# Prompt scores from float32r parts, one tile for both score banks, and a first layer with six equal PSUM banks

## The chip, the cores and the metric

The kernel runs on one core of one Trainium2 chip. The metric is the device time of one execution in microseconds (us). Three runs of the kernel before give a median of 1257.61 us (1257.02 to 1259.03). Inside the core, TensorE (PE, with weight loads as PEld), VectorE (DVE), ScalarE (ACT) and GpSimd (POOL) run side by side; SyncE (SP) issues most of the loads. PE writes into PSUM, which has eight banks; DVE and ACT read the results out of them.

## The reference, cut to what matters

Two layers run over a prompt of 512 tokens and 64 sample tokens (8 sequences of 8), so 576 columns in all, 1024 features wide. Each layer is `x + gate(c) * Mixer(RMSNorm(x) * (1 + scale(c)) + shift(c))`; shift, scale and gate come from `silu(c) @ ada_w + ada_b` (the conditioning). Layer 0 is a gated linear recurrence; layer 1 is attention with three groups of dilation 1, 4 and 16. For the prompt, in one group:

```
s = einsum('brihd,brjhd->brhij', q, k) * ATT_SCALE - slopes * (diff * dil)
s = where(valid, s, NEG_INF)
lse = logsumexp(s); p = exp(s - lse)
o = einsum('brhij,brjhd->brihd', p, v)
```

The three groups are joined by a softmax over their `lse`, which equals one softmax over all scores of the three groups. The new k and v rows of the prompt are outputs too, as are the recurrence's states. All of it is in float32.

## The kernel before

A product of two float32 matrices is made from parts: H is the value rounded to float32r (an ACT copy, line 148), L is the rest (a DVE subtraction, line 149), and PE sums H·H, H·L and L·H in three float32r matmuls. So each weight tile of 128 columns costs 8 k-tiles × 3 products × 2 halves (256 prompt columns; 256 prompt and 64 sample columns) = 48 matmuls in `project` (line 182). Matmuls on plain float32 operands stand in the trace as two matmul records each.

**First layer.** The conditioning is made in parts of 512 columns by `ada_part`: two rounds (`q` = 0 and 4) of four float32 matmuls at line 245, each on one k-tile of `ada_w`, then a DVE copy (line 215) and four small transposing matmuls (line 218). The parts of the shift and scale of layer 0 stand at the start. With `project_wide` (line 201) the first three weight tiles of the layer are accumulated beside them, k-tile by k-tile, as the modulated input `hH`, `hL` appears. Then twelve input tiles go through a convolution on DVE (`xb_group`), the gates (`gates`, line 494: matmuls into the `sc` banks, a sigmoid on ACT, then exp, tanh, sqrt on ACT and a scan on DVE, line 512), and a gating by twelve further tiles (`gb_group`). Eight further conditioning parts are called one by one between these groups by `next_ada`, a whole part each time. Then `lru_w_out` is applied (line 182 with `YH`, `YL`), the residual and the next norm follow.

**Second layer.** For each pair of heads (hp, 8 of them) nine weight tiles give q, k and v in three groups; q and k stay in tiles `qk`, features on partitions, so the two heads lie on partitions 0 to 63 and 64 to 127. `prompt_att` goes through four blocks B of 128 queries. For each head (hh) it writes the scores of group 0 (line 793, 256 keys, or 128 in block 0, float32) and of groups 1 and 2 (line 798, 32-row pieces, float32) into a bank `sc`. DVE adds the bias (lines 805, 808) and finds the maximum (line 810), ACT takes exp (line 811), PE transposes (lines 816, 818) and multiplies with v (line 826). The sample attention (`sample_att`) runs in small steps between the weight tiles, and its scores use the `sc` banks as well.

**PSUM and order.** The eight banks: `mm` 2, `tp` 2, `sc` 2, `pvp` 1, `pvs` 1. In the first layer `project` goes round `mm`, `mm`, `pvp`, `pvs`. The order on each engine is made by a scheduler from the order of the code, a priority mark (`tc.high_priority`) and its own timing model; each engine then runs its list strictly in order, and an instruction that waits holds up all behind it on its engine.

Of the kernel before, what the change touches and what calls it, by code (L numbers as in the profile page):

```python
# [26 lines left out]
TAB_W = 512 + S_W + 256 + 32 + 4 + 32 + 32 + 4 + 8 + 32 + 16  # L27
QK_BUFS = 10
# [9 lines left out]
def shape_consts():  # L38
# [41 lines left out]
    hm = 0.5 * ((np.arange(256) // 64)[None, :] == h4)  # L80
# [7 lines left out]
def kernel(  # L88
# [16 lines left out]
    def bank(tag, bufs, name):  # L105
        return ps.tile([128, 512], F32, name=name, tag=tag, bufs=bufs)

    mm_tags = ["mm", "mm", "pvp", "pvs"]
    mm_next = [0]

    def mm_bank():
        tag = mm_tags[mm_next[0] % len(mm_tags)]
        mm_next[0] += 1
        return bank(tag, 2 if tag == "mm" else 1, tag)


    tp_bank = lambda: bank("tp", 2, "tp")
    sc_bank = lambda: bank("sc", 2, "sc")
    pv_bank = lambda tag="pvp": bank(tag, 1, tag)

# [65 lines left out]
    def project_wide(raws, xs):  # L186

        pts = []
        for o in range(3):
            a = bank("mm", 2, "mm") if o < 2 else pv_bank("pvp")  # L190
            b = sc_bank() if o < 2 else pv_bank("pvs")
            pts.append((a[:, 0:256], b[:, 0:320]))
        n = len(xs)
        for q in range(0, n, 4):
            ws = [split_w(r[:, q:q + 4], 4, xs[q:q + 4])[0] for r in raws]
            for k, (XH, XL) in enumerate(xs[q:q + 4]):
                for o, (H, L, _) in enumerate(ws):
                    for half in range(2):
                        c0, c1 = CHUNKS[half]
                        for i, (a, b) in enumerate(((H, XH), (H, XL), (L, XH))):  # L200
                            T.matmul(pts[o][half], a[:, k], b[:, c0:c1], start=(q + k == 0 and i == 0),
                                     stop=(q + k == n - 1 and i == 2))
        return pts
# [29 lines left out]
    def ada_part(pool, l, f0, f1, kstep=1, abufs=4):  # L233

        pt = sc_bank()
        for q in (0, 4):
# [10 lines left out]
            with tc.issue_after(lead.ins):  # L247
                for j in range(3):
                    part(j)
        if l == 1 and f0 >= 16:  # L250
            ada_rows(pool, pt, f0)
        else:
            ada_mod(pool, l, pt, f0, f1)

# [103 lines left out]


# [19 lines left out]
    for c in range(4):  # L379
        ada_part(sp, 0, 2 * c, 8 + 2 * c, 2, 12)  # L380
        if c == 1:
            raw0 = [load_raw(lru_w_in[0, :, 128 * j:128 * (j + 1)], 8) for j in range(3)]
        for kt in (2 * c, 2 * c + 1):
            xn = sp.tile([128, NT], F32, name="xn", tag="xn", bufs=2)
            h = sp.tile([128, NT], F32, name="hmod", tag="hmod", bufs=2)
            G.tensor_tensor(xn, xT[:, kt], bc, ALU.mult)
            modulate(h, 0, kt, xn)
        if c == 3:
            nc.sync.dma_start(xs_dram[0], xT)
    wide0 = project_wide(raw0, hX)  # L390
# [20 lines left out]
    def xb_group(g, wide=None):  # L411
# [32 lines left out]
        if wide:  # L444
            def wide_evac(o, pts):
                prep(o)
                for half in range(2):
                    make(o)(half, pts[half])
                conv(o)
            for o, pts in enumerate(wide):  # L450
                wide_evac(o, pts)
        else:
            for o in range(3):
                j = 3 * g + o
                prep(o)
                project(load_w(lru_w_in[0, :, 128 * j:128 * (j + 1)], 8, hX), make(o))
                conv(o)
# [19 lines left out]
    def gates(g, xs):  # L477
# [39 lines left out]
    def gb_group(g, hs):  # L517
# [3 lines left out]
        for o in range(3):  # L521
# [8 lines left out]
            split(hs[:, o], YH[:, o], YL[:, o])  # L530
        return [(YH[:, o], YL[:, o]) for o in range(3)]

    adas = [(0, 16, 18), (0, 20, 22)] + [(1, 2 * c, 8 + 2 * c) for c in range(4)] + [(1, 16, 18), (1, 20, 22)]

    def next_ada(n=1):
        for _ in range(n):
            if adas:
                ada_part(lp, *adas.pop(0))

    yX = []  # L540
    x0 = xb_group(0, wide0)
    x1g = xb_group(1)
    m0 = gates(0, x0)
    next_ada()
    x2 = xb_group(2)
    m1 = gates(1, x1g)
    next_ada()
    yX += gb_group(0, m0)
    next_ada()
    x3 = xb_group(3)  # L550
    m2 = gates(2, x2)
    next_ada()
    yX += gb_group(1, m1)
    next_ada()
    m3 = gates(3, x3)
    next_ada()
    yX += gb_group(2, m2)
    next_ada(2)
    yX += gb_group(3, m3)
    warm = lp.tile([128, 1], F32, name="warm")  # L560
# [78 lines left out]
    mm_tags[:] = ["mm"]  # L639
# [7 lines left out]
    for w in (512, S_W, 256, 32, 4, 32, 32, 4, 8, 32, 16):  # L647
# [29 lines left out]
    def tnt():  # L677
        return ap.tile([128, NT], F32, name="qk", tag="qk", bufs=QK_BUFS)
# [25 lines left out]
    def qkv(hq, KN, VN, qs, q, k, tok):  # L704

        def make(hp, g, c):
            hpi = hp % 2
            dst = t512("vT", 2) if c == 2 else tnt()

            def pevac(half, pt):  # L710
                cs = slice(256 * half, 256 * half + 256)
                if c == 0:
                    S.activation(dst[:, cs], pt[:, 0:256], AF.Copy, scale=0.125)
                else:
                    order = "p (b s r) -> p b r s" if g == 0 else "p (r b s) -> p b r s"
                    evac(dst[:, 0:NP].rearrange(order, b=4, r=4)[:, 2 * half:2 * half + 2],
                         pt[:, 0:256].rearrange("p (b r s) -> p b r s", b=2, r=4))
# [7 lines left out]
        def after(hp, g, c, dst):  # L725
# [6 lines left out]
            if g == 0:  # L732
# [8 lines left out]
                else:  # L741
                    T.transpose(tp[:, 0:128], dst[:, 384:512], eye)
# [22 lines left out]
        if hq == 0:  # L765
            def wide_evac(o, pts):
                dst, f = make(0, 0, o)
                for half in range(2):
                    f(half, pts[half])
                after(0, 0, o, dst)  # L770
            raws = [load_raw(att_w_in[0, :, 1024 * c:1024 * c + 128], 8) for c in range(3)]
# [489 lines left out]
```

## Time and profile before

| | |
|---|---|
| median of three runs | 1257.61 us |
| the profiled execution | 1252.48 us, of which the span of the instructions is 1250.7 us |
| PE, DVE, ACT busy | 1182.4, 844.9, 448.7 us |
| PE share of the chain that ended last | 82% |
| mean granted clock of PE | 0.969 of full speed |

The span is the time from the first to the last instruction of the program; the rest of the execution lies around it. The chain that ended last is found backwards from the last instruction: at each step to what released it, or to the instruction before it on its engine. A stretch that it spends on a DMA or on "issue" is time in which PE stood still. The granted clock of PE has two levels, 1.2 and 2.4 GHz; 1.00 means that the upper one held throughout the stretch.

### The profile page before, as it was taken

To read this page: it belongs to the slowest core of one execution; us is meant where nothing else is said; L and a number is where in the kernel's file an instruction comes from. 1 tells how busy PE (TensorE), PEld (TensorE's weight loads), DVE (VectorE), ACT (ScalarE), POOL (GpSimd) and SP (SyncE) were. 2 spreads that over 40 slices of the span, in tenths; PEclk is the share of its full clock that TensorE was granted. 3 is DMA by queue.
4 is the path that set the end of the run, shared out by engine and by line. 5 is a ranking of instruction groups with operands and counts; after the bars stand their busy time and mean duration, and the time that the engine had idled before them with its cause. 6 is when DMAs were issued, how large, how long until landed. Compare 5 with 4: busy or idle time off the path is not lost.

```text
span 1250.7 us, 25771 instructions
## 1 busy us (share of the span) xinstructions
PE 1182.4 (95%) x10344; PEld 1038.2 (83%) x10344; DVE 844.9 (68%) x1609; ACT 448.7 (36%) x895; POOL 219.2 (18%) x299
## 2 busy tenths in 40 slices
PE   6989899898997999899999999999999999999897
PEld 4789889786897998797998897988887988897775
DVE  6585894835437349885588765687774777776645
ACT  4167566552322323233222333223232223233421
POOL 3234453522110201020010030020020100030000
PEclk9899999997997999899999999999999999999899
DMA  9742253445540488482699481999671997484912
GB/s 302 232 117 89 82 169 91 147 125 178 156 137 27 128 225 224 131 241 79 181 262 237 132 243 52 251 252 203 185 199 56 269 255 173 124 231 145 239 55 76
DMA packets 242565, 209.51 MB, mean 168 GB/s; under 512 B 15324, under 2 KB 224956, under 8 KB 242318
## 3 DMA queue, kind: packets, MB, share of 16 engines
q1 hardware_dynamic: 229218, 172.73, 50.5%
q10 hardware_dynamic: 8124, 23.61, 6.4%
q0 software_dynamic: 5104, 11.52, 3.1%
q8 instruction: 82, 1.34, 0.5%
q14 instruction: 37, 0.30, 0.1%
HBM read 188.94 MB, written 18.87 MB: 166 GB/s over the span
## 4 chain that ended last, share of the span: by engine, by line
PE 82%; DMA 7%; DVE 6%; issue 2%; ACT 2%; SPq 0%; POOL 0%; ACTq 0%; DVEq 0%; POOLq 0%
PE mm L182 44%; PE mm L1191 4%; PE pvs L182 4%; PE pvp L182 4%; PE pvs L1011 3%; PE sc L494 3%; PE sc L793 3%; PE sc L798 2%; PE pvp L826 2%; PE sc L245 2%; DMA adaw<-in_ada_w_dram 2%; DMA q<-q2d 1%; PE tp L749 1%; PE tp L816 1%; PE tp L818 1%
## 5 line engine op out<-in xcount | busy, mean ns | idle before, releaser
L182 PE MATMUL mm<-hH,wH 128*128 128x256 f32 (+1 forms) x1392 | 424.8, 305 | 4.3 <-ACT wH L148 1.3
L182 PE MATMUL mm<-hL,wH 128*128 128x256 f32 (+1 forms) x1392 | 417.2, 300 | 0.0
L182 PE MATMUL mm<-hH,wL 128*128 128x256 f32 (+1 forms) x1392 | 416.3, 299 | 0.0
L182 PEld LDWEIGHTS mm<-hH,wH 128*128 128x128 f32 x1392 | 264.2, 190 | 22.7 <-issue 12.1
L182 PEld LDWEIGHTS mm<-hL,wH 128*128 128x128 f32 x1392 | 264.5, 190 | 6.2 <-issue 5.5
L149 DVE TENSOR_TENSOR wL<-wraw,wH 128x512 fp32r<-128x512 f32 (+1 forms) x240 | 167.4, 700 | 149.4 <-ACT wH L148 143.4
L182 PEld LDWEIGHTS mm<-hH,wL 128*128 128x128 f32 x1392 | 264.2, 190 | 3.8 <-issue 3.3
L148 ACT ACTIVATE wH<-wraw 128x512 fp32r<-128x512 f32 (+1 forms) x244 | 149.9, 617 | 295.1 <-PE mm L182 215.6
L811 ACT ACTIVATE p<-p,nm 128x192 f32<-128x192 f32 (+3 forms) x64 | 38.9, 608 | 36.4 <-DVE nm L810 35.6
L752 POOL DMA_DIRECT2D out_dram<-tok x32 | 23.1, 730 | 150.7 <-DVE tok L672 68.5
L745 POOL DMA_DIRECT2D out_dram<-kn x8 | 4.5, 568 | 251.8 <-ACT kn L670 142.3
L924 DVE TENSOR_TENSOR kvc<-kvc,q 128x1024 f32<-128x1024 f32 x32 | 39.0, 1219 | 11.9 <-DMA kvc<-in_cache_kv_g_dram 9.3
L670 ACT ACTIVATE PT<-tp 128x256 f32<-128x256 f32 (+4 forms) x64 | 23.5, 368 | 59.0 <-DVE PT L672 27.5
L1011 PE MATMUL pvs<-vrow,pT 128*32 128x256 f32 x512 | 41.8, 386 | 1.9 <-DMA vrow<-in_cache_kv_g_dram 1.9
L932 DVE TENSOR_TENSOR pr<-kvc,q 128x1024 f32<-128x1024 f32 x32 | 38.9, 1217 | 2.0 <-DMA q<-q1d 1.2
L441 DVE SCALAR_TENSOR_TENSOR XC<-xpad,vecT,XC 128x512 f32<-128x512 f32 (+1 forms) x72 | 37.2, 570 | 3.5 <-ACT XC L439 3.5
L932 DVE TENSOR_TENSOR kvc<-kvc,q 128x1024 f32<-128x1024 f32 x32 | 39.2, 1224 | 0.0
L925 DVE TENSOR_REDUCE R<-kvc 128x16 f32<-128x1024 f32 x32 | 38.7, 1210 | 0.1
L933 DVE TENSOR_REDUCE R<-pr 128x16 f32<-128x1024 f32 x32 | 38.7, 1210 | 0.1
L933 DVE TENSOR_REDUCE R<-kvc 128x16 f32<-128x1024 f32 x32 | 38.7, 1210 | 0.0
L798 PEld LDWEIGHTS sc<-qk 64*32 64x32 f32 x1024 | 18.5, 107 | 21.5 <-issue 19.6
L672 DVE COPY PT<-tp 128x256 f32<-128x256 f32 (+4 forms) x64 | 25.4, 399 | 16.0 <-PE tp L818 12.8
(423 smaller groups left out, 2414.7 us busy)
## 6 DMA issues: line engine op xcount, KB each, us to landing
wraw<-in_att_w_in_dram SPq DMA_DIRECT2D x80, 512.0 KB, 5.2
kvc<-in_cache_kv_g_dram SPq DMA_DIRECT2D x48, 512.0 KB, 5.5
adaw<-in_ada_w_dram SPq DMA_DIRECT2D x64, 256.0 KB, 5.1
kvc<-in_cache_kv_g_dram SPq DMA_DIRECT2D x128, 128.0 KB, 5.9
vrow<-in_cache_kv_g_dram SPq DMA_DIRECT2D x32, 512.0 KB, 8.0
vrow<-in_cache_kv_g_dram SPq DMA_DIRECT2D x64, 256.0 KB, 8.1
wraw<-in_lru_w_in_dram SPq DMA_DIRECT2D x24, 512.0 KB, 4.7
adaw<-in_ada_w_dram SPq DMA_DIRECT2D x64, 128.0 KB, 3.4
```

Source lines behind the costliest of these rows:

```text
L148: S.activation(H, x, AF.Copy)
L149: V.tensor_tensor(L, x, H.bitcast(F32), ALU.subtract)
L182: T.matmul(pt, a[:, k], b[:, c0:c1], start=(i == 0), stop=(i == 3 * n - 1))
L494: T.matmul(pt, w[:, pc], x[:, c0:c1], start=(n == 0), stop=(n == 5))
L798: T.matmul(sc[hh][32 * r:32 * r + 32, w0 + (g - 1) * w1:w0 + g * w1], q[g][rows_[hh], 128 * B + 32 * r:128 * B + 32 * r + 32], k[g][rows_[ ...
L811: S.activation(p[:, 0:W], p[:, 0:W], AF.Exp, bias=nm[:, 0:1], accum_out=nm[:, 1:2])
L924: V.tensor_tensor(kr, kr, q2[:, i:i + 1].broadcast_to([128, 4, 256]), ALU.mult)
L925: V.tensor_reduce(R2[:, i], kr.rearrange("p j (h d) -> p j h d", h=4), axis=AX.X, op=ALU.add)
L932: V.tensor_tensor(pr, kr, q1[:, c:c + 1].broadcast_to([128, 4, 256]), ALU.mult)
L933: V.tensor_reduce(R1[:, i, :, :, u], pr.rearrange("p j (h d) -> p j h d", h=4), axis=AX.X, op=ALU.add)
L1011: T.matmul(pv[32 * b:32 * b + 32, 0:256], pT[:, 4 * g - 2 + c, 32 * b:32 * b + 32], vr[:, b], start=False, stop=(g == 2 and c == 3), skip_ ...
L1191: T.matmul(pt[0:N], a[:, k, ts], b, start=(n == 0), stop=(n == 23))
```

## The change

- **Group 0 of the prompt scores.** q and k of group 0 are kept as float32r parts (ACT copy for H, DVE subtraction for L, read from PSUM), so each product is three float32r matmuls (`two_sc`, new line 841) in place of one float32 matmul. The last 128 keys are also copied as they are (`kf`), for the output of new rows. The tiles `qk` are 512 columns wide and there are 12 of them.
- **Both score banks are one tile.** `two_sc` takes two neighbouring banks as one tile; the matmuls of the two heads stand in turn and carry the priority mark. The sample scores and the conditioning sums now use `tp` banks.
- **First layer.** Six equal banks `mm` serve projections and gates. `load_wide` and `project_wide` take four first tiles, in steps of two k-tiles. The chain of small operations for `csp` stands behind the wide tiles.
- **Conditioning in halves.** `ada_part` is a generator that yields after each round of four matmuls; `next_ada` does one such half after each weight tile of `xb_group` (from the fifth on) and of `gb_group` (first three groups).
- The head mask is 4 columns and broadcast; `ym` shares the buffers of `PT0`.

The core of the diff:

```diff
-QK_BUFS = 10
+QK_BUFS = 12
-    mm_tags = ["mm", "mm", "pvp", "pvs"]
+    mm_bufs = [6]
+    mm_bank = lambda: bank("mm", mm_bufs[0], "mm")
+    def two_sc():
+        t = bank("sc", 1, "sc", 1024)
+        return t[:, 0:512], t[:, 512:1024]
...
+        for q in range(0, 8, 2):
+            ws = []
+            for g in groups:
+                a, per = g[0].shape[2], g[0].shape[1]
+                H, L = (wp.tile([128, 4, 128], F32R, name=t, tag=t, bufs=4)[:, 0:2 * a]
+                        .rearrange("p (k a) c -> p k a c", a=a) for t in ("wH", "wL"))
+                split(g[q // per][:, q % per:q % per + 2], H, L)
...
     def ada_part(pool, l, f0, f1, kstep=1, abufs=4):
-        pt = sc_bank()
+        pt = tp_bank()
...
+            if not q:
+                yield
...
+            raw0 = load_wide([lru_w_in[0, :, 128 * j:128 * (j + 1)] for j in range(4)],
+                             sp.tile([128, 8, 128], F32, name="raw3"))
...
+    def next_ada():
+        while adas:
+            if next(adas[0], adas) is not adas:
+                return
+            adas.pop(0)
...
-                    pt = sc_bank()[:, :c1 - c0]
+                    pt = mm_bank()[:, :c1 - c0]
...
+                if g == 0 and c == 0:
+                    H, L = (t[:, cs] for t in dst)
+                    S.activation(H, pt[:, 0:256], AF.Copy, scale=0.125)
+                    V.scalar_tensor_tensor(L, pt[:, 0:256], 0.125, H.bitcast(F32), ALU.mult, ALU.subtract)
+                elif g == 0 and c == 1:
+                    H, L, kf = dst
+                    S.activation(nat(H), blocks(pt[:, 0:256]), AF.Copy)
+                    V.tensor_tensor(nat(L), blocks(pt[:, 0:256]), nat(H.bitcast(F32)), ALU.subtract)
...
-            sc = [sc_bank() for _ in range(2)]
-            for hh in range(2):
-                T.matmul(sc[hh][:, 0:w0], q[0][rows_[hh], 128 * B:128 * B + 128],
-                         k[0][rows_[hh], 128 * (B + 1) - w0:128 * (B + 1)], start=True, stop=True)
+            sc = two_sc()
+            with tc.high_priority():
+                for i, (a, b) in enumerate(((0, 0), (0, 1), (1, 0))):
+                    for hh in range(2):
+                        T.matmul(sc[hh][:, 0:w0], q[0][a][rows_[hh], 128 * B:128 * B + 128],
+                                 k[0][b][rows_[hh], 128 * (B + 1) - w0:128 * (B + 1)], start=(i == 0), stop=(i == 2))
...
-        sc = sc_bank()
+        sc = tp_bank()
```

How the order on PE moves is seen at two places. First the end of the input side of the first layer, where `lru_w_out` (operands `YH`, `YL`) begins. Before, on PE:

```order
L182 MATMUL pvs<-hL,wH 128x320
L182 MATMUL pvs<-hH,wL 128x320
L245 MATMUL sc<-adaw,cT 32x512 x4
L218 MATMUL tp<-small,adap 128x10 x4
L182 MATMUL mm<-YH,wH 128x256
L182 MATMUL mm<-YL,wH 128x256
L182 MATMUL mm<-YH,wL 128x256
```

After, on PE, at the same place (line 183 is the projection's matmul now):

```order
L183 MATMUL mm<-hH,wH 128x320
L183 MATMUL mm<-hL,wH 128x320
L183 MATMUL mm<-hH,wL 128x320
L183 MATMUL mm<-YH,wH 128x256
L183 MATMUL mm<-YL,wH 128x256
L183 MATMUL mm<-YH,wL 128x256
```

The conditioning part in front of `YH` is gone; the last conditioning matmuls (line 272) stand 178 projection matmuls further up, between projections. Between the last gate matmul and `YH` there are 288 projection matmuls now, where there were 42.

Second, the scores of one block of 128 queries in the second layer (the first head pair, block 2 and 3). Before, on PE:

```order
L793 MATMUL sc<-qk 128x256
L798 MATMUL sc<-qk 32x128 x8
L826 MATMUL pvp<-PT_5087,tok 64x128
L826 MATMUL pvp<-PT_5071,tok 64x128
L826 MATMUL pvp<-PT_5087,tok 64x128
L793 MATMUL sc<-qk 128x256
L798 MATMUL sc<-qk 32x128 x8
L816 MATMUL tp<-small,p 128x128 x2
```

After, on PE (lines 841 and 846 are the two score matmuls, 865 and 867 the transposes of `p`, 875 the product with v):

```order
L841 MATMUL sc<-qk 128x256 x6
L846 MATMUL sc<-qk 32x96 x16
L865 MATMUL tp<-small,p 128x128 x2
L867 MATMUL tp<-small,p 64x128 x2
L865 MATMUL tp<-small,p 128x128 x2
L867 MATMUL tp<-small,p 64x128 x2
L875 MATMUL pvp<-PT_5105,tok 64x128
L875 MATMUL pvp<-PT_5121,tok 64x128
L875 MATMUL pvp<-PT_5105,tok 64x128
L875 MATMUL pvp<-PT_5121,tok 64x128
L841 MATMUL sc<-qk 128x256 x6
L846 MATMUL sc<-qk 32x128 x16
```

Before, the two heads stand apart with other work between; after, six score matmuls of both heads stand together, and all small score pieces of both heads behind them. In all 24 blocks with 256 keys it is so (in the 8 blocks with 128 keys the small pieces come later, in two lots of 8). In front of 22 of these 24 score groups projection matmuls stand; in front of two (the second one shown, and one more) only eight transposes and four products stand behind the scores of the block before.

## Rows read from the trace of the kernel before

**Rows 1.** The page, part 1: busy us (share of the span) xinstructions.

```profile
PE 1182.4 (95%) x10344; PEld 1038.2 (83%) x10344; DVE 844.9 (68%) x1609; ACT 448.7 (36%) x895; POOL 219.2 (18%) x299
```

**Rows 2.** By stretch: us, busy PE, PEld, DVE, ACT, POOL; PE clock, DMA, GB/s.

```profile
25.00:65.00 40.00, 35.10 (x212) 29.35 (x204) 25.11 (x53) 10.45 (x18) 9.80 (x6) 0.79 0.73 230
65.00:280.00 215.00, 197.58 (x1425) 184.67 (x1424) 152.67 (x261) 131.37 (x215) 93.17 (x95) 0.98 0.40 117
280.00:300.00 20.00, 12.57 (x68) 9.73 (x68) 11.49 (x17) 6.52 (x11) 7.50 (x12) 0.66 0.43 138
...
422.00:1155.00 733.00, 725.53 (x7154) 631.77 (x7151) 527.38 (x980) 222.41 (x506) 79.94 (x149) 0.99 0.70 186
```

**Rows 3.** PE's waits, 65 to 300 us: total us, times, longest us.

```profile
PE sc L245 <- DMA adaw<-in_ada_w_dram: 6.8, 5, 3.3
PE mm L182 <- DVE sg L527: 4.9, 2, 3.7
PE sc L494 <- ACT IG L496: 4.3, 1, 4.3
...
PE tp L218 <- DVE adap L215: 2.9, 3, 1.9
```

**Rows 4.** The chain that ended last, 64 to 78 us: start us, us, what.

```profile
66.02 6.66 PE mm L182 x48
72.67 4.00 issue
76.67 0.51 PE sc L494 x2
```

**Rows 5.** In order of time, 41 to 56 us: start us, us, engine, instruction.

```profile
45.63 1.06 PE L245 MATMUL sc<-adaw,cT 128*32 128x512 f32 x8
...
53.52 1.26 ACT L148 ACTIVATE hH<-hmod 128x576 fp32r<-128x576 f32 x2 [5.57 <-DVE hmod L297]
```

**Rows 6.** The chain, 422 to 1155 us: shares of these 733 us by line.

```profile
by line: PE mm L182 62.4%; PE pvs L1011 4.5%; PE sc L793 4.4%; PE sc L798 3.9%; PE pvp L826 3.5%; DMA q<-q2d 2.3%; PE tp L749 2.0%; PE tp L816 2.0%; PE tp L818 1.8%; DMA kvc<-in_cache_kv_g_dram 1.7%; DMA vrow<-in_cache_kv_g_dram 1.4%; PE pv
```

**Rows 7.** The chain, pieces with scores: start us, us, what.

```profile
421.77 0.42 PE sc L793 x4
...
474.22 0.63 PE sc L793 x2
474.85 0.34 PE sc L798 x10
...
475.81 0.36 PE sc L798 x21
...
770.67 0.63 PE sc L793 x4
771.31 0.38 PE sc L798 x16
...
1050.82 0.48 PE sc L798 x28
```

**Rows 8.** The chain, 82 to 89 us: float32r matmuls of 320 and of 256 columns.

```profile
82.34 3.52 PE pvs L182 x24
85.86 2.88 PE pvp L182 x24
```

**Rows 9.** Line 793's weight loads: ns minimum/median/maximum, first and last start us, form.

```profile
L793 PEld LDWEIGHTS sc<-qk x128: 182/186/334, 421.7 to 1142.2; 64*128 64x128 f32 x128
```

**Rows 10.** DVE groups, 422 to 1155 us: count, busy us, mean ns, idle before.

```profile
L805 DVE SCALAR_TENSOR_TENSOR p<-tab,sc 128x256 f32<-128x256 f32 x48 | 19.9, 414 | 8.9 <-PE tp L818 4.4 <-PE sc L798 4.3
...
L672 DVE COPY qk<-mm 128x256 f32<-128x256 f32 x23 | 11.1, 482 | 7.3 <-PE mm L182 6.1 <-PE sc L793 1.2
...
L810 DVE TENSOR_REDUCE nm<-p 128x1 f32<-128x448 f32 x16 | 9.4, 608 | 0.1
...
L941 DVE SCALAR_TENSOR_TENSOR Sb<-tab,sc 128x224 f32<-128x224 f32 x7 | 3.1, 445 | 1.5 <-PE sc L961 1.5
```

**Rows 11.** PE's waits, 422 to 1155 us: total us, times, longest us.

```profile
PE pvp L826 <- DVE PT L672: 3.1, 1, 3.1
```

More of the change, by code (lines that the diff above doesn't have):

```diff
@@ L184, in project, with load_wide, rawt, fill @@
             evac(half, pt)
[L186 to L197, printed above, removed]
+    def load_wide(cols, last=None):
+        def rawt():
+            return wp.tile([128, 8, 128], F32, name="wraw", tag="wraw", bufs=3)
+        def fill(raw, srcs, k0, k1):
+            for a, src in enumerate(srcs):
+                nc.sync.dma_start(raw[:, :, a], src[128 * k0:128 * k1].rearrange("(k p) c -> p k c", p=128))
+            return raw
+        pair = lambda t: t.rearrange("p (k a) c -> p k a c", a=2)
+        groups = [[fill(pair(rawt()), cols[0:2], 0, 4)], []]
+        if len(cols) == 3:
+            groups[1] = [fill(rawt().unsqueeze(2), cols[2:], 0, 8)]
+        else:
+            groups[1] = [fill(pair(rawt()), cols[2:], 0, 4)]
+        groups[0].append(fill(pair(rawt()), cols[0:2], 4, 8))
+        if len(cols) == 4:
+            groups[1].append(fill(pair(last), cols[2:], 4, 8))
+        return groups
+    def project_wide(groups, xs):
+        n = sum(g[0].shape[2] for g in groups)
+        halves = [mm_bank() for _ in range(2)]
+        rest = [mm_bank() for _ in range(n)] if mm_bufs[0] == 6 else [*two_sc(), pv_bank()]
+        pts = [(halves[o // 2][:, 256 * (o % 2):256 * (o % 2) + 256], rest[o][:, 0:320]) for o in range(n)]
+        for q in range(0, 8, 2):
[5 more added lines that the diff above has]
+                split(g[q // per][:, q % per:q % per + 2], H, L)
+                ws += [(H[:, :, i], L[:, :, i]) for i in range(a)]
+            for k, (XH, XL) in enumerate(xs[q:q + 2]):
+                for o, (H, L) in enumerate(ws):
                     for half in range(2):
@@ L200, in project_wide @@
                         for i, (a, b) in enumerate(((H, XH), (H, XL), (L, XH))):
-                            T.matmul(pts[o][half], a[:, k], b[:, c0:c1], start=(q + k == 0 and i == 0),
-                                     stop=(q + k == n - 1 and i == 2))
+                            first = q + k == 0 and i == 0 and (half == 1 or o % 2 == 0)
+                            T.matmul(pts[o][half], a[:, k], b[:, c0:c1], start=first,
+                                     stop=(q + k == 7 and i == 2), skip_group_check=True)
         return pts
@@ L442, in conv @@
             split(xc[:, o], xH[:, o], xL[:, o])
-        if wide:
-            def wide_evac(o, pts):
-                prep(o)
+        for o in range(3):
+            j = 3 * g + o
+            prep(o)
+            if j < 4:
                 for half in range(2):
[L448 to L455, printed above, removed]
+                    make(o)(half, wide0[j][half])
+            else:
                 project(load_w(lru_w_in[0, :, 128 * j:128 * (j + 1)], 8, hX), make(o))
-                conv(o)
+            conv(o)
+            if j > 3:
+                next_ada()
         return xc, xH, xL
@@ L637 @@
     lsm.close()
-    mm_tags[:] = ["mm"]
+    sums.close()
+    sum_pool[0] = ctx.enter_context(tc.tile_pool(name="sums1", bufs=1, space=PSUM))
+    mm_bufs[0] = 2
     att = ExitStack()
@@ L715, in pevac @@
                     order = "p (b s r) -> p b r s" if g == 0 else "p (r b s) -> p b r s"
[L716 to L717 removed]
+                    evac(dst[:, 0:NP].rearrange(order, b=4, r=4)[:, 2 * half:2 * half + 2], blocks(pt[:, 0:256]))
                 if half and c == 0:
```

119 lines of the change are left out of this document (61 added, 58 removed).

## The prediction

> **What bounds the kernel now.** I read the page's busy shares first, then busy time by stretch, then the chain that ended last, and PE's waits stretch by stretch. PE is the engine with the most work [rows 1]. By stretch it differs: from 422 to 1155 us, the second layer, PE is busy 725.5 of 733 us at a clock of 0.99, DVE 527.4 (72%) and ACT 222.4 [rows 2], and PE's longest wait there is one of 3.1 us [rows 11]; a microsecond less on PE is there nearly a microsecond less in the end. The first layer is looser: 35.1 of 40 us at a clock of 0.79 from 25 to 65 us, 197.6 of 215 us to 280, and only 12.6 of 20 us at 0.66 from 280 to 300 [rows 2]. There the waits of PE are the thing to read [rows 3]: for conditioning weights (6.8 us), for a PSUM bank that a gating step still reads (4.9), for a sigmoid that frees a gate bank (4.3), for the copy of a conditioning sum (2.9), and 4.0 us in front of the first gates [rows 4].
>
> **The change, part by part.**
>
> *Prompt scores.* Now: the chain gives line 793 4.4% and line 798 3.9% of 733 us [rows 6], which is 32.3 and 28.6 us, 60.9 together. Where a head stands alone, its 256-key product takes 0.63 us (two records), so two heads 1.26; where the two stand together, four records take 0.63, since the heads sit on different halves of the array's rows [rows 7]. So standing together is worth half already. The float32r parts: a matmul of 256 columns takes 2.88 / 24 = 0.120 us in the stream, one of 320 columns 3.52 / 24 = 0.147 [rows 8]. No row shows a float32r matmul on 64 rows. If the two heads run beside each other as the float32 ones do, the six take 3 × 0.12 = 0.36 us; if they don't, 6 × 0.12 = 0.72. I take 0.36, since rows 7 show this very pair of operands overlapping, and nothing but the type differs. Blocks of 128 keys take 0.42 now [rows 7]; after, 0.36 at most. Line 841: 32 × 0.36 = 11.5 us instead of 32.3. The small pieces: 32 records per block. With both heads in turn 28 records of 96 columns take 0.48 us and 21 of 64 columns 0.36, 17 ns each, and 16 of 128 columns 0.38; a head alone takes 0.34 for 10 of 64 [rows 7]. So 0.55, 0.55, 0.76 for 64, 96, 128 columns, and 0.55 at most for 32: 2.4 us per head pair, 8 × 2.4 = 19.3 us instead of 28.6. Sum 30.8 instead of 60.9: **30 us less PE time**; with 0.72 for the six 19 us, and at best, with the small pieces still shorter, 33.
>
> What it adds: per head pair DVE subtracts four halves of 256 (q and k), against one half of k that it copied before, and copies 128 keys. With 0.48 us for such a read of PSUM [rows 10] that is 3 × 0.48 + 0.24 = 1.7 us, 14 us for eight; ACT gains eight short copies. The cover is PE: DVE goes from 527 to 541 of about 710 us, 76%, and stays under it. New waits: one tile for both banks means that block B + 1 can't start before DVE has read both heads of block B: 2 × (0.41 + 0.35) + 0.61, about 2.1 us with the reduce between [rows 10]; the 0.35, for the second read with fewer columns, is an estimate from the first. Behind such a wait stand all of PE's matmuls. In 22 of 24 places projections stand in front, which cover it; in two only about 1.5 us of transposes and products do, and I charge 1.5 us each, 3 us. The sample scores take `tp` banks, 16 tiles, with a DVE read of 0.45 us at their end (line 941) [rows 10]; I charge 0.3 us each, 5 us. From both sides: nothing if other work stands between, 16 × 2 us if each holds up a transpose and its copy. Net for the second layer: 30 - 8 = **22 us**; range 5 to 33.
>
> *Four first tiles.* The last modulated input is written by ACT at 53.52 + 1.26 = 54.8 us [rows 5]. Its conditioning weights come 0.52 MB later in the queue, at 230 GB/s [rows 2] 2.3 us: 57.1. Of the 192 first-tile matmuls the new order leaves 90 behind the last conditioning; with a mean of (2.88 + 3.52) / 48 = 0.133 us [rows 8] they end at 69.1. Two further tiles, 96 matmuls, end at 81.9, two conditioning rounds of 1.06 us [rows 5] at 84.0; then the first gates, with six tiles done. Before, the gates start at 76.7 with four tiles done, after a wait of 4.00 us (the gates' weights and the split of the convolution, ACT and DVE work) [rows 4]; two more tiles and two rounds make 76.7 + 12.8 + 2.1 = 91.6. Gain **7.6 us**. What would take it back: the convolution of the first three tiles, the splits of two weight tiles and of the gate weights are all DVE's, and now fall into 15 us; then the gates wait as before, and 4 us of the gain go.
>
> *Conditioning in halves, six equal banks.* The weights of the second round are loaded while a projection runs, and are used a tile later: the 6.8 us can go. The gates have six banks: the 4.3 us can go. The copy of a sum has some 25 to 45 matmuls in front of its transposes: the 2.9 us can go. At the end of the input side the last gates have 288 projection matmuls behind them, 38 us, where 42 were; the scan, the gating and the bank that PE waited 4.9 us for are then long done [rows 3]. Sum 18.9 us. The clock of 0.66 in 280 to 300 means (1 - 0.66) / 0.5 = 68% of the stretch at 1.2 GHz; of 12.6 us of work 8.5 ran at half speed, 4.3 us lost, which go with the idle time. With the 7.6 us that is 30.8. DVE at 153 and ACT at 131 of 215 us [rows 2] run in order too, and a wait that is taken away often meets the next: I take three quarters, **23 us**; range 8 to 31.
>
> *With one answer.* The moved `csp` chain, the mask and `ym` change no more than a few small operations off PE's path. The first tiles of the second layer are the same three, split in smaller steps: nothing.
>
> **A rule of the skill against this.** Each of line 793's loads lasts 182 to 186 ns, and yet two heads take no longer than one, and a full-height float32r matmul with its load 0.12 us [rows 7 to 9]: loads hide behind the other head's or the previous matmul. The Trainium skill (TensorE: Matmul & The Clock Gate, LDWEIGHTS) says that a load's time goes with its columns alone, so that a half-height load costs as much as a full one; by its formula an estimated 107 ns for 128 columns, and if loads go one by one, 213 ns per pair of heads, 640 ns for the six. By that the sum of the second layer would be some 8 us smaller. The rows of float32 pairs speak against it, no row of float32r pairs exists.
>
> **The rivals.** (a) *The loads set the pace*: six float32r matmuls take what the float32 pair takes, 0.63 us (0.42 in the small blocks); line 841 then costs 24 × 0.63 + 8 × 0.42 = 18.5 us, 7 more: 1219 us. For it: twice as many loads on half the rows. Against it: rows 8. (The skill's load rule, above, comes to the same time.) (b) *The first layer's waits only move*: DVE and ACT, in order, are what PE waits for; only 8 of the 31 us go: 1227 us. For it: DVE at 71% from 65 to 280 us, with scans and gates in lumps. Against it: the longest waits are for DMA and for banks. (c) *All of it comes*: 33 and 31 us: 1194 us. (d) *Slower*: the score tile and the `tp` banks, now shared by the sample scores, become the chain of the second layer. If each of the 24 score groups holds PE for the 3.1 us that it once waited for a `PT` [rows 11], that is 74 us against a gain of 45 + 3, and the time 1284. It decides from 48 / 24 = 2 us per group; the projections in front of 22 of them speak against it. (e) *It doesn't do what it says*: the built order shows the parts together and the halves apart, so this is left only as the gain being spent elsewhere (DVE or DMA at 186 GB/s setting the second layer): about 1257.
>
> **How the numbers follow.** Profiled execution 1252.5, less 22 and 23: 1207.5. The median before is 5.1 us above the profiled execution; with that 1212.6, said as **1212 us**. Chances: forecast (1200 to 1217) 0.45; (a) 0.14; (b) 0.16; (c) 0.13; (d) 0.07; (e) 0.05. The range from 1190 to 1236 takes in (a), (b) and (c) with some width and leaves out (d) and (e). A measurement of this kernel can tell about 0.2% from no change: faster 0.89, same 0.03, slower 0.08.
>
> **What would show it.** In the profile after: line 841's six records per block in 0.4 us (0.63 or more shows rival a, 0.72 no overlap at all); lines 841 and 846 with some 31 us of the chain; PE busy over 98% in the second layer with no wait above 3 us in front of scores or transposes (else d); the first gates near 84 us with no stop before them; no stretch of the first layer behind 65 us at a clock under 0.9, and PE's waits for `adaw` near nothing (else b). The second layer should start some 23 us earlier and last some 22 us less. I would be wrong in kind if DVE came over 90% of the second layer, or if PE's waits there summed to over 20 us.

## The result, and the profile after

The changed kernel takes 1211.36 us (median of 4 runs, 1209.06 to 1220.04) against 1257.32 before (4 runs): ratio 0.965, interval 0.960 to 0.970. The forecast was 1212. The total is right to a microsecond, and that is luck: in the table below the first layer gives 9 us more than forecast, the second 7 less, and the output stage takes 3 that no term had.

The profiled execution took 1209.59 us (span 1207.4). Against the one before (span 1250.7) the 43.3 us fall like this; the borders are the last matmul of the second layer's first tiles and the first of `att_w_out`:

| stage | before | after | difference | forecast |
|---|---|---|---|---|
| to the end of the second layer's first tiles | 414.5 | 382.6 | -31.9 | -23 |
| second layer from there | 757.7 | 743.1 | -14.6 | -22 |
| output stage | 78.5 | 81.7 | +3.2 | 0 |

Busy time by stretch of the kernel after, with the columns of [rows 2]; the stretches moved, so the last one is the second layer from the end of its first tiles:

```profile
25.00:65.00 40.00, 38.88 (x281) 30.80 (x280) 29.57 (x70) 13.65 (x25) 13.65 (x12) 0.96 0.94 287
65.00:280.00 215.00, 206.93 (x1515) 188.33 (x1508) 171.84 (x278) 133.48 (x219) 94.04 (x102) 0.99 0.47 138
280.00:300.00 20.00, 20.00 (x155) 19.83 (x154) 6.55 (x16) 8.71 (x15) 3.50 (x5) 1.00 0.40 118
383.00:1126.00 743.00, 724.32 (x7504) 645.28 (x7505) 547.53 (x1036) 235.86 (x533) 82.79 (x155) 0.99 0.67 189
```

PE's clock from 25 to 65 us is 0.96 where it was 0.79, and the stretch from 280 to 300 us, busy for 12.6 of 20 us at 0.66 in [rows 2], is full and all at the upper level. The clock moves from one execution to the next (a second profiled execution of the changed kernel, experiment 5, has 0.92 from 25 to 65 us), but the two profiles with the old first layer have 0.79 and 0.76 (experiment 2). The second layer has 18.7 us in which PE stands. Its longest waits and a short one, and below them those of the first layer (65 to 383 us), as total, times, longest:

```profile
PE tp L865 <- DVE p L862: 4.4, 1, 4.4
PE mm L183 <- DVE qk L757: 4.1, 3, 1.7
PE pvs L1060 <- DMA vrow<-in_cache_kv_g_dram: 3.1, 3, 1.7
PE tp L790 <- DVE KN L769: 2.6, 2, 1.5
...
PE sc L841 <- DVE p L857: 0.2, 1, 0.2
```

```profile
PE mm L228 <- ACT hH L149: 5.1, 2, 3.8
PE tp L272 <- DMA adaw<-in_ada_w_dram: 3.2, 4, 1.0
PE tp L245 <- DVE adap L242: 2.7, 1, 2.7
```

Of the waits in [rows 3], `sg` (4.9) is gone, that for `IG` (4.3) is 0.8, `adaw` (6.8) is 3.2, `adap` (2.9) is 2.7. In the second layer `qk L757` (the new subtraction, which holds a projection's bank) and `KN` (a DVE copy that stands behind the new ones) are new.

**The block of scores.** PE in order of time, one block of 256 keys; columns: start, us, line, count:

```profile
641.52 0.62 PE L841 MATMUL sc<-qk 64*128 64x256 f32 x6
642.07 0.56 PE L846 MATMUL sc<-qk 64*32 64x96 f32 x32
642.56 0.33 PE L865 MATMUL tp<-small,p 128*128 128x128 f32 x1
```

Read the starts, since ends are modelled. The six matmuls take 642.07 - 641.52 = 0.55 us (mean over the 24 blocks 0.553), between the forecast 0.36 and rival (a)'s 0.63. Summed over PE's rows, from each start to the next, lines 793 and 798 took 32.0 + 28.5 = 60.5 us before; lines 841 and 846 take 17.1 + 24.1 = 41.2, of which 8.5 us are waits that follow directly behind a lot (an unbroken run) of small pieces. Without these the scores cost 17.1 + 15.6 = 32.7 us of PE's time.

### The profile page after: what moved, and what is told of

Same layout as the page of the kernel before. It is cut to its first block, busy times and chain, and to the rows that moved or that the text cites. A ratio compares the mean times of both kernels' runs of the same rounds, so it can differ in the third digit from the quotient of the medians.

```text
span 1207.4 us, 25932 instructions
## 1 busy us (share of the span) xinstructions
PE 1148.5 (95%) x10408; PEld 1019.3 (84%) x10408; DVE 856.4 (71%) x1643; ACT 449.8 (37%) x904; POOL 213.9 (18%) x299
## 5 line engine op out<-in xcount | busy, mean ns | idle before, releaser
L183 PE MATMUL mm<-hH,wH 128*128 128x320 f32 (+1 forms) x1552 | 473.3, 305 | 5.2 <-DVE qk L757 4.1
L183 PE MATMUL mm<-hH,wL 128*128 128x320 f32 (+1 forms) x1552 | 466.3, 300 | 0.0
L183 PE MATMUL mm<-hL,wH 128*128 128x320 f32 (+1 forms) x1552 | 465.7, 300 | 0.0
L183 PEld LDWEIGHTS mm<-hH,wH 128*128 128x128 f32 x1552 | 296.3, 191 | 26.4 <-issue 11.8
L183 PEld LDWEIGHTS mm<-hL,wH 128*128 128x128 f32 x1552 | 296.5, 191 | 6.3 <-issue 6.0
L183 PEld LDWEIGHTS mm<-hH,wL 128*128 128x128 f32 x1552 | 296.1, 191 | 6.5 <-issue 5.3
L150 DVE TENSOR_TENSOR wL<-wraw,wH 128x512 fp32r<-128x512 f32 (+1 forms) x240 | 159.8, 670 | 119.3 <-ACT wH L149 115.9
L860 ACT ACTIVATE p<-p,nm 128x192 f32<-128x192 f32 (+3 forms) x64 | 38.9, 609 | 35.8 <-DVE nm L859 34.6
L183 PE MATMUL mm<-YL,wH 128*128 128x256 f32 (+1 forms) x144 | 42.7, 296 | 0.0
L183 PE MATMUL mm<-YH,wH 128*128 128x256 f32 (+1 forms) x144 | 42.6, 296 | 0.0
L183 PE MATMUL mm<-YH,wL 128*128 128x256 f32 (+1 forms) x144 | 42.5, 295 | 0.0
L981 DVE TENSOR_TENSOR pr<-kvc,q 128x1024 f32<-128x1024 f32 x32 | 38.9, 1217 | 0.1
```

The costliest lines, as they stand in the source:

```text
L150: V.tensor_tensor(L, x, H.bitcast(F32), ALU.subtract)
L183: T.matmul(pt, a[:, k], b[:, c0:c1], start=(i == 0), stop=(i == 3 * n - 1))
L860: S.activation(p[:, 0:W], p[:, 0:W], AF.Exp, bias=nm[:, 0:1], accum_out=nm[:, 1:2])
L981: V.tensor_tensor(pr, kr, q1[:, c:c + 1].broadcast_to([128, 4, 256]), ALU.mult)
```

## The experiments

Two theories stood at the start. **A**, from the table above: the first layer gives 32 us, the second 11 with the output stage, and DVE's in-order queue with the new subtractions takes the rest back. **B**: the prediction's split, 23 and 22 us, in which the float32r parts are worth the 7 us that separate it from its rival (a). The kernels were timed in five groups (1 to 4; 5 to 8; 9 to 11; 12; the changed kernel itself), each beside the kernel before on its chip, whose medians were 1255.6 to 1260.3 us; across groups the ratios are compared.

**1 and 2. Each half alone.** `e1_first_only` puts the second layer back to its state before (plain q and k, two score tiles, heads apart); `e2_second_only` does so with the first layer. In short, on the changed kernel:

```diff
-        t = bank("sc", 1, "sc", 1024)
-        return t[:, 0:512], t[:, 512:1024]
+    sc_bank = lambda: bank("sc", 2, "sc")
```

```diff
-    mm_bufs = [6]
+    mm_tags = ["mm", "mm", "pvp", "pvs"]
...
-            if not q:
-                yield
```

> The first layer as changed, the second as before (plain float32 scores, heads apart, two score tiles, sample scores in them). Theory A, from comparing the two traces by stage: the first layer gives 32 us, so 1257 - 32 = 1225 (1222 to 1229). Theory B, the prediction's split: it gives 23 us, so 1234, and the rest of the gain needs the second layer. Theory C: the stages trade with each other, and the first layer alone gives neither, under 18 us (above 1239).

Measured: 1221.91 us, ratio 0.976 (0.971 to 0.981).

> The first layer as before, the second as changed. Theory A (traces by stage): 14.6 us less in the second layer and 3.2 more behind it, so 11 us, 1246 (1242 to 1249). Theory B (prediction's split): 22 us, 1235. Theory C: above 1250, the parts of the scores give nothing unless the stage starts earlier. If A holds for both, the two gains sum to the whole, 32 + 11 = 43 of 46.

Measured: 1241.72 us, ratio 0.991 (0.988 to 0.995). The first layer gives 30 to 34 us, the second 11 to 14; the two shares, 2.4 and 0.9%, sum to 3.3 of the 3.5%. Theory A's split holds; the prediction's 22 us for the second layer lies outside the interval of experiment 2 (6 to 15 us).

**3. The parts taken out, everything else kept.**

```diff
-                for i, (a, b) in enumerate(((0, 0), (0, 1), (1, 0))):
-                    for hh in range(2):
-                        T.matmul(sc[hh][:, 0:w0], q[0][a]..., k[0][b]..., start=(i == 0), stop=(i == 2))
+                for hh in range(2):
+                    T.matmul(sc[hh][:, 0:w0], q[0]..., k[0]..., start=True, stop=True)
```

> As changed, but q and k of group 0 stay plain float32: one score matmul for each head and block (two records), both heads side by side in the one score tile, no subtractions on DVE, no extra copy of the last 128 keys. Theory A: the parts themselves give little, since six of them took 0.55 us where two heads of plain float32 side by side took 0.63 before; 24 x 0.08 = 2 us lost on TensorE, and some of the 10 us of new waits for DVE comes back: 1205 to 1213. Theory B: the parts take 0.36 against 0.63, and their loss costs 24 x 0.27 + 8 x 0.06 = 7 us: 1218. Theory C: with plain float32 the heads don't run side by side as well as they did in the blocks seen before, above 1222.

Measured: 1201.27 us, ratio 0.957 (0.953 to 0.962). Faster than the changed kernel by some 9 us, and beyond what any theory allowed. One block of it:

```profile
636.59 0.70 PE L823 MATMUL sc<-qk 64*128 64x256 f32 x4
637.23 0.56 PE L828 MATMUL sc<-qk 64*32 64x96 f32 x32
```

Both heads in plain float32 take 0.64 us, so the six float32r matmuls save 0.08 us per block of 256 keys (means 0.63 and 0.55): 18.6 us against 17.1 for all 32 blocks. That is all the parts give. The same second layer by busy time (columns of [rows 2]), and below it PE's longest waits there:

```profile
387.00:1119.50 732.50, 720.26 (x7440) 639.04 (x7440) 537.11 (x1009) 233.71 (x528) 83.66 (x155) 0.99 0.68 192
```

```profile
PE mm L183 <- DVE qk L703: 4.4, 1, 4.4
PE mm L183 <- issue: 2.7, 1, 2.7
PE mm L183 <- ACT vT L701: 1.3, 1, 1.3
PE sc L828 <- DVE qk L703: 1.2, 1, 1.2
```

PE stands 12.2 us instead of 18.7, and is busy 4 us less, though its scores cost 1.3 us more (34.0 against 32.7 without waits). The output stage is 78.0 us again.

**4. The other copies off DVE.** `evac` always uses ACT in the second layer.

```diff
-        flip[0] ^= 1
-        if flip[0]:
-            S.activation(dst, src, AF.Copy)
-        else:
-            V.tensor_copy(dst, src)
+        S.activation(dst, src, AF.Copy)
```

> As changed, but the copies out of PSUM in the second layer that go to ScalarE and VectorE in turn all go to ScalarE (32% busy there). Theory A: TensorE's 18 us of waits in the second layer come from DVE's queue, in order, where the new subtractions stand among the softmax steps; with the copies gone from it the waits fall by half and the time is 1201 to 1206. Theory B: the waits are the length of the chain score, bias, maximum, exp, scale, transpose, copy, whatever engine does the copy; the time stays within 1209 to 1214. Theory C: ScalarE's queue is now what holds, slower than 1216.

Measured: 1214.81 us, ratio 0.968 (0.964 to 0.973). DVE's busy time falls from 856 to 804.5 us and nothing is gained: theory A's reason, a full DVE queue, doesn't hold for these copies; the time is nearest to theory B.

**5 and 6. The subtractions left out.** `e5_changed_again` is the changed kernel, for comparison on one chip.

> The changed kernel itself, timed on the same chip as the three kernels that follow, so that they can be compared with it. Ratio to before 0.965 (0.960 to 0.970), some 1211 us, if the chip doesn't matter.

Measured: 1210.76 us, ratio 0.9645 (0.961 to 0.968).

```diff
-                dst = [tnt().bitcast(F32R) for _ in range(2)]
+                dst = [tnt().bitcast(F32R)] * 2
...
-                    V.scalar_tensor_tensor(L, pt[:, 0:256], 0.125, H.bitcast(F32), ALU.mult, ALU.subtract)
...
-                    V.tensor_tensor(nat(L), blocks(pt[:, 0:256]), nat(H.bitcast(F32)), ALU.subtract)
```

The score of group 0 is then three times the product of the high parts.

> As changed, but the low part of q and k in group 0 isn't computed: the three products take the high part in its place, so TensorE does the same six matmuls for each block, and DVE's 32 subtractions out of PSUM (14 us of its time) are gone. The scores of group 0 are then wrong in their low bits. Theory A, after plain float32 scores (four matmul records, no subtraction) were 10 us faster than the parts: it is the subtractions, which stand in DVE's order among the softmax steps and hold the projection's bank; without them 1198 to 1203. Theory B: it is the form of the matmuls (changes between operand types or tile sizes on TensorE), which stays: 1208 to 1213. Theory C: it is half and half, 1203 to 1208.

Measured: 1214.92 us, ratio 0.968 (0.964 to 0.972): no gain. Its waits in the second layer:

```profile
PE pvs L1058 <- DMA vrow<-in_cache_kv_g_dram: 8.8, 4, 3.8
PE tp L863 <- DVE p L860: 5.8, 3, 5.2
PE tp L788 <- DVE KN L767: 1.7, 1, 1.7
```

The wait for `qk L757` is gone, as theory A had it, and PE's busy time falls to 721 us; but PE stands 20.0 us, with 8.8 for cache rows, where the changed kernel's two profiled executions have 3.1 and 4.4. So one wait goes, others are longer in this execution, and nothing is gained in the time. What makes the form with parts 9 us slower isn't settled: the runs exclude the subtractions alone, and the matmuls themselves are 1.5 us faster. The added copies, the two further `qk` buffers and the order that the scheduler builds for them remain, and no run told these apart.

**7. Two score tiles.** On the kernel of experiment 3:

```diff
-        t = bank("sc", 1, "sc", 1024)
-        return t[:, 0:512], t[:, 512:1024]
+        return [bank("sc", 2, "sc") for _ in range(2)]
```

> The kernel with plain float32 scores (1201 us, ratio 0.957), and the two banks of scores as two tiles rather than one, the heads' matmuls still in turn with the priority mark. Theory A: what gains is that the heads' matmuls stand in turn, the single tile adds only a wait for the second head's reads, so two tiles are the same or a little faster: 1197 to 1203. Theory B: the single tile is what keeps the two heads together and so gains; with two the scheduler draws the heads apart again where one bank is free earlier, and the time goes towards 1222, what the old score code gives with the new first layer: 1208 to 1222.

Measured: 1229.24 us, ratio 0.981 (0.977 to 0.984), 28 us worse than experiment 3 and past theory B's end. The code still writes the heads in turn and gives them the priority mark. PE, one block:

```profile
641.64 0.70 PE L822 MATMUL sc<-qk 64*128 64x256 f32 x2
642.27 0.53 PE L827 MATMUL sc<-qk 64*32 64x96 f32 x16
642.73 0.63 PE L1041 MATMUL pvs<-vrow,pT 128*32 128x256 f32 x6
...
644.08 0.70 PE L822 MATMUL sc<-qk 64*128 64x256 f32 x2
644.70 0.53 PE L827 MATMUL sc<-qk 64*32 64x96 f32 x16
```

One head: 0.63 us, and 0.46 for its small pieces. The next head, 2.4 us later, pays both again. In experiment 3 two heads together take 0.64 and 0.49. A likely reason, which no run shows by itself, is that the bank of one head comes free before the other's, and the scheduler puts that head's scores in first. Lots of line 822 start 61 times instead of 32; score matmuls of group 0 cost 35.5 us instead of 18.6, the small pieces 24.4 instead of 15.4 (without the waits behind them). Together that is 59.9 us, as much as the old score code takes with the new first layer (experiment 1: 60.8), against 34.0 with one tile. **The second layer's gain hangs on the single tile, which lets no head go ahead of the other.** The priority mark, the heads in turn and the sample scores in `tp` stand in this kernel too and alone gain nothing; whether the single tile would gain without them, no run shows.

**8. The six products twice.**

```diff
-                for i, (a, b) in enumerate(((0, 0), (0, 1), (1, 0))):
+                for i, (a, b) in enumerate(((0, 0), (0, 1), (1, 0)) * 2):
...
```

> As changed, with the six score matmuls of group 0 issued twice over in each block (the second round overwrites the first). Theory A: in the trace the pairs of heads start 0.22, then 0.12 us apart, and the small pieces 0.21 behind the last; so a pair of products costs 0.11 to 0.12 as the prediction had it, and the other 0.2 us is a load that nothing covers where the tile size changes, once at each end. Six more products then cost 24 x 0.35 + 8 x 0.25 = 10 us: the twelve take 0.90 us, the time is 1219 to 1224. Theory B: the pairs cost 0.18 us each wherever they stand: 24 x 0.55 + 8 x 0.48 = 17 us, the twelve take 1.1 us, 1226 to 1231.

Measured: 1218.58 us, ratio 0.971 (0.967 to 0.976).

```profile
640.30 0.98 PE L841 MATMUL sc<-qk 64*128 64x256 f32 x12
641.21 0.56 PE L846 MATMUL sc<-qk 64*32 64x96 f32 x32
```

Twelve take 0.91 us, six more cost 0.36: **0.12 us for each pair**, just what the prediction took. The other 0.19 us of the six belong to the ends. In the trace of the changed kernel the pairs start at 0, 0.22 and 0.34 us and the small pieces at 0.55: about 0.1 us more behind the first pair and 0.1 behind the last. Theory A, if just under its range.

**9 and 10. The first layer's parts undone.** `e9_whole_conditioning` runs a conditioning part as a whole at every second call; `e10_gate_banks` gives the gates two banks of their own and leaves four to the projections.

```diff
-            if not q:
-                yield
...
+        turn[0] += 1
-        while adas:
+        while adas and turn[0] % 2 == 0:
```

> As changed, but a conditioning part is done as a whole at every second call (both rounds of four matmuls one behind the other) rather than one round at each call. Theory A, the prediction's step: the second round then waits for its weights, whose four buffers come free only with the first round, and the 6.8 us of waits for adaw and some of the 2.9 us for the copy come back: the first layer ends 6 to 10 us later, the time is 1217 to 1221. Theory B: with the calls spread over the projections the loads are covered anyway and it was the place of the parts, not the halves, that counted: 1209 to 1214.

Measured: 1214.19 us, ratio 0.967 (0.963 to 0.971). Waits for `adaw` 4.5 us instead of 3.2, the first layer ends at 385.8 us. At the upper end of theory B: the halves are worth some 3 us by the ratios, which isn't told apart from nothing.

```diff
-    mm_bufs = [6]
+    mm_bufs = [4]
...
-                    pt = mm_bank()[:, :c1 - c0]
+                    pt = bank("gate", 2, "gate")[:, :c1 - c0]
```

> As changed, but of the six equal banks of the first layer two serve the gates alone and four the projections. Theory A, the prediction's step: the wait of 4.3 us for a sigmoid that frees a gate bank comes back, with smaller ones in the other three gate groups (12 sums each in two banks): 4 to 8 us, 1215 to 1219. Theory B: what freed PE was the place of the gate groups among projections, and two banks do as well: 1209 to 1213.

Measured: 1217.71 us, ratio 0.9675 (0.964 to 0.971): in theory A's range, but 4 us by the ratios and not told apart from the changed kernel's 0.9645, and not for theory A's reason. In its profiled execution, the slowest of its six, the first layer ends 9 us later, but its waits for gate sums that ACT still reads come to 2.6 us, against 1.5 in the changed kernel. Most of the rest is a lower clock (0.88 from 25 to 65 us, 0.96 behind it), which also differs between two executions of one kernel.

**11. An improved version.** On the kernel of experiment 3 the transposes of `p` of both heads stand together, behind the second head's softmax:

```diff
+            with tc.high_priority():
+                lead = T.transpose(*jobs[0], eye)
+                with tc.issue_after(lead.ins):
+                    for j in jobs[1:]:
+                        T.transpose(*j, eye)
```

> The kernel with plain float32 scores in one tile (1201 us, ratio 0.957), with the transposes of p of both heads of a block put together behind the second head's softmax. In the traces each change of TensorE from one kind of matmul to another takes about 0.2 us where the steps within a kind take 0.02 to 0.12; the built order has 79 fewer such changes. Theory A: that is what made one tile for both heads gain (80 fewer changes, 18 to 28 us), and each change is worth 0.1 us or more: 8 us or more less, 1188 to 1194. Theory B: the first head's transposes wait for the second head's softmax on DVE, and TensorE gets new waits that eat the gain: 1199 to 1210.

Measured: **1197.70 us, ratio 0.951 (0.948 to 0.954)**, 17 us under the changed kernel by the ratios and the fastest here. With both heads' `p` transposed at once, the products with v come in 43 lots instead of 69, and PE changes its kind of work (projection, scores, transposes, products) some 500 times in the second layer instead of 580. The second layer takes 724.8 us against 732.7. Both theories are in these 8 us: PE's work fell by 16 us (720.5 to 704.5, of which 9.1 on the products with v), and its waits rose by 8 (12.2 to 20.3). The output stage went from 78.0 to 82.5. By the ratios the total gained 8 us over experiment 3, by the medians, from two chips, 3.6; the two intervals touch, so this step is only just clear of noise. My expectation was wrong in one thing: what experiment 7 lost is mostly the second head's own time, not the changes (scores 26 us of the 33 by which its second layer is longer in the profiles).

**12. Three first tiles.**

```diff
-            raw0 = load_wide([lru_w_in[0, :, 128 * j:128 * (j + 1)] for j in range(4)],
-                             sp.tile([128, 8, 128], F32, name="raw3"))
+            raw0 = load_wide([lru_w_in[0, :, 128 * j:128 * (j + 1)] for j in range(3)])
```

> As changed, but with three first tiles rather than four in the first layer; the fourth comes behind them as a projection of its own. Theory A, after the trace showed a clock of 0.92 to 0.96 from 25 to 65 us where the kernel before has 0.79: the fourth tile's 48 matmuls fill TensorE while the conditioning weights arrive and keep its clock up; without them the clock there falls towards 0.8, the first gates start 5 us or more later and the first layer ends 5 to 8 us later: 1216 to 1220. Theory B: the steps of two k-tiles and the later place of the gates do it, the fourth tile only changes which matmuls stand first: 1209 to 1214.

Measured: 1210.87 us, ratio 0.962 (0.959 to 0.966). Theory B: the fourth tile gives nothing that shows in the total. By stretch:

```profile
25.00:65.00 40.00, 33.98 (x239) 27.84 (x239) 26.66 (x65) 10.20 (x19) 13.25 (x9) 0.91 0.83 257
65.00:386.00 321.00, 307.57 (x2225) 286.20 (x2224) 220.43 (x403) 169.78 (x287) 113.20 (x117) 0.97 0.44 131
```

PE does less up to 65 us and its first gates start at 84.7 us instead of 79.5, and yet the first layer's stage ends at 386.0, against 382.6 and 384.4 in the two profiled executions of the changed kernel: less idle time behind 65 us makes up for it.

## Why the prediction held, and which of its steps failed

**The first layer was undervalued by 9 us.** Its sum before the discount, 30.8, is near what came (31.9), so as a number the step that failed is the discount ("I take three quarters"). But that is a coincidence too, for the terms inside are not what the sum says; the one most undersized is the clock. The stretch from 65 us to the end of the stage, in the kernel before and then in the one after:

```profile
65.00:415.00 350.00, 316.81 (x2244) 294.20 (x2244) 221.11 (x410) 172.00 (x287) 114.48 (x120) 0.95 0.41 123
```

```profile
65.00:383.00 318.00, 302.11 (x2192) 281.52 (x2184) 220.83 (x398) 166.19 (x279) 107.83 (x115) 0.97 0.43 129
```

With [rows 2] and its counterpart after for 25 to 65 us, PE stood 4.9 + 33.2 = 38.1 us before and 1.1 + 15.9 = 17.0 after: 21 us. An estimate of the busy time lost at the lower clock, busy time by one less the granted clock, is 35.1 × 0.21 + 316.8 × 0.05 = 23 us before and 38.9 × 0.04 + 302.1 × 0.03 = 11 after: some 12 us, where the prediction charged 4.3 for one stretch alone. Of the four waits that it summed to 18.9, 6.7 are left (3.2, 2.7 and 0.8), so 12 went; the halves, charged 6.8 + 2.9, took 3.8 of it. The first gates start at 79.5 us, with the six tiles and two rounds of the prediction's count done, 12.1 us before the prediction's 91.6 for the old order, where it had 7.6; yet of what the fourth tile adds to that, experiment 12 finds nothing in the total. Undone one at a time, halves, banks and the fourth tile cost 3, 4 and 0 us by the ratios, each within its interval of nothing; they don't sum to 32. That the first layer's edits together give the 30 to 34 us is shown (experiment 1); which of them does is open. They may stand in for each other, or the place of the conditioning (none in front of `lru_w_out` any more) does most. No run told these apart.

**The second layer was overvalued by 7 us.** PE's busy time between the table's borders, before (after it was 724.3 of 743.0 us):

```profile
415.00:1172.00 757.00, 746.76 (x7437) 651.84 (x7436) 541.11 (x1008) 232.88 (x527) 83.77 (x155) 0.99 0.70 187
```

So PE's work fell by some 23 us, not 30, and its waits rose by the 8 that were charged: from 10.2 to 18.5 us, counting those of 0.15 us and more. Term by term, from start to start without these waits:
- Line 841: 17.1 us instead of 11.5; this is the term that was mis-sized. The pair of products at 0.12 us is right, heads beside each other too (experiment 8); what was left out is 0.1 us at each end of a lot. The plain form's 0.63 us in [rows 7] is read from start to start as well, so it has its ends in it; 0.36 had none. Of the 7 us that the prediction gave the parts 1.5 came.
- Small pieces: 15.6 us, 3.7 less than the 19.3 forecast. In all the scores gave 27.8 us of the 30 forecast.
- PE's other work grew by 5.0 us (686.9 to 691.9), for which the sum had no term; 3.3 of that are the sample products with cache rows (line 1060). Why they take longer is open. With the waits: 27.8 - 5.0 - 8.2 = 14.6.
- Waits: 8 us charged, 8.2 came, but not where they were charged. The score tile was charged 3, and PE's wait for it is 0.2 (line 841 for `p L857`); the sample scores in `tp` were charged 5, and no wait of PE names a read of them. In their place stand waits for DVE in its order, for `p`, `qk`, `KN` and `vT`. The longest falls into one of the two places without projections, but it is the transposes that wait there, for the softmax:

```profile
458.15 0.56 PE L846 MATMUL sc<-qk 64*32 64x96 f32 x32
463.09 0.66 PE L865 MATMUL tp<-small,p 128*128 128x128 f32 x2 [4.38 <-DVE p L862]
```

DVE at the same time: between the scores and the scaling of `p` it runs key steps (lines 974 and 982) and weight splits (line 150), in order.

```profile
457.96 1.21 DVE L974 TENSOR_REDUCE R<-kvc 128x16 f32<-128x1024 f32 x1
459.09 0.68 DVE L150 TENSOR_TENSOR wL<-wraw,wH 128x512 fp32r<-128x512 f32 x1
459.69 1.00 DVE L859 TENSOR_REDUCE nm<-p 128x1 f32<-128x384 f32 x2
...
461.21 1.21 DVE L982 TENSOR_REDUCE R<-kvc 128x16 f32<-128x1024 f32 x1
...
462.52 0.75 DVE L862 TENSOR_SCALAR p<-p,nm 128x384 f32<-128x384 f32 x2
```

- The single tile: the prediction charged its wait and took the heads' standing together as given. Experiment 7 shows that in this kernel it hangs on the tile: 28 us are lost with two.

**The loads, and the ends of a lot.** Each load of line 841 lasts 182 to 188 ns (count and minimum/median/maximum):

```profile
L841 PEld LDWEIGHTS sc<-qk x192: 182/185/188, 389.3 to 1098.5; 64*128 64x128 f32 x192
```

Yet a pair of heads costs 0.12 us within a lot (experiment 8). If loads went one by one, as the prediction's estimate from the Trainium skill (TensorE: Matmul & The Clock Gate, LDWEIGHTS) had it, six would take 640 ns; the trace doesn't agree, and rival (a) falls with it, though its price was near. Another page would explain both ends: by the Trainium skill (TensorEngine Tiling (Array Packing), Key Properties) tiles of the array load and multiply in parallel, and a change of the tiling mode drains TensorE. The trace agrees with both: 0.12 us a pair, some 0.1 us at each end of a lot, and (medians over PE's rows of the changed kernel's second layer) 0.20 to 0.31 us from start to start where a projection on 128 × 128 gives way to a score, a product with v or a sample product on narrower tiles, or one of these products to a projection, against 0.03 to 0.15 between projections and transposes, most of which keep the size. From a small score piece to a projection it is 0.12. Whether the ends are this or a first load that nothing covers, which experiment 8 named, no run separates. The prediction didn't weigh that page, and it bore on the term that was mis-sized.

**The signs that the prediction named.** First gates at 79.5 us (84 was said), no stop of 4 us before them. One stretch behind 65 us lies under a clock of 0.9: 0.88 from 320 to 360 us, around the norm at the end of the layer. `adaw` at 3.2 us, not near nothing. PE 97.5% busy in the second layer instead of 98, with one wait of 4.4 us in front of transposes where none above 3 was to be; waits of 18.7 us, just under the 20 that would have been wrong in kind (a second profiled execution has 19.9). The output stage's 3.2 us had no term; PE waits there once, 4.8 us, for a weight split on DVE (line 150), where it was 2.4 before.

## What to carry to other kernels

When an edit bundles a new arithmetic form with a new grouping, cost each from the rows apart: here two heads side by side already had a price in the trace before, the new form could save only a part of that, and a kernel with the grouping alone beats the bundle. Where an in-order engine gets two independent halves of one step, binding their buffers into one tile can be worth more than the freedom of two. Sum the lost clock over all stretches, not only over the slowest one. When a total fits, compare the stages before believing the terms: here two errors of opposite sign met.

## What the runs showed of the hardware

Two heads on different halves of PE's rows cost about the time of one (experiments 3 and 7): 0.64 against 0.63 us for plain float32 scores, 0.49 against 0.46 for the small pieces. A pair of float32r products of two heads costs 0.12 us in a lot (experiment 8). The ends of a lot cost about 0.1 us each: in the changed kernel it takes 0.21 us from the last pair of scores to the first small piece (median), where the pairs themselves are 0.12 apart. A wait taken away came back elsewhere: without the subtractions the wait for `qk` went from 4.1 us to nothing, and that for cache rows from 3.1 to 8.8 (one execution of each).
